# Sliding-window attention on one core: one masking with a difference of values, moved transposes and low parts, and another order of its end

## The chip, the core and the metric

The program runs on one core of a Trainium2 chip. Five engines work side by side, each through its own instructions in program order: TensorE (PE) multiplies matrices, VectorE (DVE), ScalarE (ACT) and GpSimd (POOL) work on elements, and SyncE (SP) issues most transfers. They wait for each other by semaphores. The metric is the device time of one execution in microseconds (us); the median of three runs before is 2189.2, from 2187.97 to 2191.01.

## The reference

A trunk of two layers over 1024 tokens of width 1024. The first layer mixes tokens by a gated linear recurrence, the second by the attention that the change touches; each is followed by a normalisation and a gated feed-forward block. The attention has 16 query heads and 4 shared key and value heads of 64. A query block of 128 tokens sees its own block and the one before, and of these only the 128 newest positions:

```python
t = jnp.arange(SW_WINDOW)[:, None] + SW_WINDOW
s = jnp.arange(2 * SW_WINDOW)[None, :]
dist = t - s
band = (dist >= 0) & (dist < SW_WINDOW)
...
logits = jnp.where(mask[None, :, None, None], logits, -jnp.inf)
m = jnp.maximum(logits.max(-1), sink)
p = jnp.exp(logits - m[..., None])
denom = p.sum(-1) + jnp.exp(sink - m)
o = jnp.einsum('bngrts,bnsgd->bntgrd', p, vv.astype(jnp.float32))
o = o / jnp.moveaxis(denom, -1, 2)[..., None]
```

So in a row of 256 logits exactly 128 count: of the own block the positions up to the query, of the previous block the positions behind it. Both halves fit into one square of 128 x 128.

## The kernel before

Large products are made in three: an operand is split into a high part (a cast on ACT) and a low part (what the cast lost, a subtraction on DVE, line 166), and high x high, high x low and low x high are summed (`mm3`, lines 191 to 193). Scores take a high and a low part of the keys; the attention's transposes (`tr`, line 201) and its products with the values (`mm32`, line 197) are in plain f32.

The attention runs over 8 values of `c` (a pair of query heads, one of each of two key heads) and 4 values of `bp` (two blocks of 128 tokens each): 32 steps, numbered here 0 to 31 as 4c + bp. `attend` is a generator that makes one step's work in seven stages:

1. scores on PE (line 1290) into a `psax` tile; ACT copies the own block's half to `X` (1293);
2. DVE lays the previous block's half over it where it counts (1297), POOL adds the bias (1303);
3. DVE takes the maximum (1308, 1311), ACT the exponentials with their sums (1315, 1317);
4. DVE adds the sink, takes the reciprocal and normalises `X` (1319 to 1321);
5. PE transposes the four squares of `X` into a `psmm` tile;
6. DVE multiplies this with each of two triangular masks (1329): `W[:, 0]` is the own block's part, `W[:, 1]` the previous block's;
7. PE multiplies with the values of the own and of the previous block (1338, 1340), ACT copies the result to column `c` of `Y` (1342), or for c = 7 splits it into `T` at once.

Four blocks are in flight. In a step the newest goes through stages 1 and 2, and the older ones through 3 and 4, 5 and 6, and 7. PE has a filler beside this: the projection of the next pair's queries (`q_proj`, two pieces of six products a step), and for c = 7 the beginnings of the output projection (`last_filler`). A finished half of the queries is split by `q_split` (1274, 1276) in every second step. `make_lows` lets out the low parts that were put off in `lows`: those of weights (`HL`), and in the last six steps those of finished columns of `Y`, which `Y_to_T` splits into `T` (`moves` says which columns in which step).

PE, ACT, DVE and POOL keep the order in which the code calls them here (`manual_schedule`), so the order of the `stage` calls in the step loop (lines 1408 to 1440) sets what stands behind what in each queue. After the loop the three blocks left over, 29 to 31, are finished by hand (lines 1441 to 1464), with pieces of the output projection (`out_part`) between their stages.

Of the kernel before, what the change touches and what calls it, by code (L numbers as in the profile page):

```python
# [10 lines left out]
F32 = mybir.dt.float32  # L11
# [5 lines left out]
P = 128  # L17
# [18 lines left out]
def constant_arrays():  # L36
    s = np.arange(P)[:, None]
    t = np.arange(P)[None, :]
    masks = np.zeros((P, 7 * BL + P), np.float32)
    bs, bt = s % BL, np.arange(BL)[None, :]  # L40
    pair = lambda m: (bs // (2 * m) == bt // (2 * m)) & (bs % (2 * m) < m) & (bt % (2 * m) >= m)
    parts = [bs == bt, pair(1), pair(2) & (bs % 4 == 0), pair(2) & (bs % 4 == 1)] + [pair(1 << i) for i in range(2, 5)]
    for i, part in enumerate(parts):
        masks[:, i * BL:(i + 1) * BL] = part
    masks[:, 7 * BL:] = t > s
    tri = np.zeros((P, 2, P), np.float32)
    tri[:, 0] = s <= t
    tri[:, 1] = s > t
    onehot = np.zeros((32, 2 * P), np.float32)
    for x in range(2 * P - 1):  # L50
        onehot[BUCKETS[(x - P + 1) % P], x] = 1.0
    return {"masks": masks, "tri": tri, "onehot": onehot}
# [55 lines left out]
def trunk(ctx: ExitStack, tc: tile.TileContext, a: dict, out: bass.AP):  # L108
# [87 lines left out]
    def mm32(ps, lhsT, rhs, start=True, stop=True, cost=0.218, **kw):  # L196
        nc.tensor.matmul(ps, lhsT, rhs, start=start, stop=stop, **kw)  # L197
        od.t += cost

    def tr(ps, src):  # L200
        nc.tensor.transpose(ps, src, ident)  # L201
        od.t += 0.109
# [989 lines left out]
    with (tc.tile_pool(name="ta", bufs=1, reuse_waits="tile") as raws,  # L1192
          tc.tile_pool(name="at", bufs=1, reuse_waits="tile") as at):
        raw_tail(raws)
        Kh = at.tile([P, 2, 2, S], F32R, name="Kh")
        tri = at.tile([P, 2, P], F32, name="tri")
# [4 lines left out]
        wkvv = wkv.rearrange("(kc p) c -> p kc c", p=P)  # L1201
        Kl = at.tile([P, 2, S], F32R, name="Kl")
        Vt = at.tile([P, NB, 256], F32, name="Vt")
        khl, uv = [], []
        for c in range(2):
            hl = split_into(hl_at(4 + c), load(lambda r: [(r.rearrange("p (k c) -> p k c", k=KC),
# [22 lines left out]
        def v_part(tp):  # L1229
            ps = psmm()  # L1230
            proj_tok(uv, tp, ps)
            nc.scalar.copy(Vt[:, 2 * tp:2 * tp + 2, :], ps.rearrange("p (a b) -> p a b", a=2))

        wq = a["swa_w_q"][0].rearrange("(kc p) (h e) -> p kc h e", p=P, e=64)

        W0 = at.tile([P, 2, 4, P], F32, name="W0")
        bfs = {}

        def bias_load(c):
# [39 lines left out]
        def attend(c, bp, q):  # L1279
# [43 lines left out]
            pt = psmm()  # L1323
            for i in range(4):
                tr(pt[:, i * P:(i + 1) * P], X[:, i // 2, i % 2, :])
            yield
            W = W0 if bp % 2 else Y[:, NB - 1, :].rearrange("p (k g s) -> p k g s", k=2, g=4)
            for k in range(2):
                nc.vector.tensor_tensor(W[:, k], pt.rearrange("p (g s) -> p g s", g=4),
                                        tri[:, k, :].unsqueeze(1).to_broadcast([P, 4, P]), op=ALU.mult)  # L1330
            yield
            po = psmm()
            for jj in range(2):
                j = 2 * bp + jj
                for e in range(2):
                    kvc = (2 * pp + e) * 64
                    o = po[64 * e:64 * e + 64, jj * P:(jj + 1) * P]
                    mm32(o, Vt[:, j, kvc:kvc + 64], W[:, 0, 2 * e + jj, :], stop=j == 0)
                    if j:
                        mm32(o, Vt[:, j - 1, kvc:kvc + 64], W[:, 1, 2 * e + jj, :], start=False)  # L1340
            if c < 7:
                nc.scalar.copy(Y[:, c, bp * 256:(bp + 1) * 256], po[:, :256])
            else:
                ts = slice(bp * 256, (bp + 1) * 256)
                split(T[:, 0, c, ts], T[:, 1, c, ts], po[:, :256], lows)
            yield

        wo2 = a["swa_w_out"][0]
# [32 lines left out]
        with tc.manual_schedule(engines={EN.PE, EN.Activation, EN.DVE, EN.Pool}):  # L1381
# [26 lines left out]
            for c in range(8):  # L1408
                fill = q_proj(hl) if c < 7 else last_filler()
                nq, nd = next(fill)  # L1410
                for bp in range(4):
                    it = attend(c, bp, q)
                    prev = [None] * (3 - len(flight)) + flight
                    if 4 * c + bp in moves:
                        Y_to_T(*moves[4 * c + bp], lows)
                    stage(it)
                    stage(prev[0])
                    stage(prev[2])
                    stage(it)
                    stage(prev[1])  # L1420
                    stage(prev[1])
                    stage(fill)
                    stage(prev[2])
                    while done:
                        q_split(*done.pop(0))
                    make_lows()
                    if bp == 0 and c < 6:
                        hl = q_unit(c + 2)
                    stage(fill)
# [69 lines left out]
```

## Time and profile before

| what | us |
|---|---|
| median of three runs | 2189.2 |
| the profiled execution | 2192.32 |
| its span | 2190.5 |
| the attention's steps 0 to 31 and its end (1276.0 to 1466.7 of the span) | 190.7 |
| PE busy in the whole span | 2168.1 |
| DVE busy in the whole span | 1762.2 |
| ACT busy in the whole span | 895.3 |

The profile is a page on one execution, with views of its trace. A timeline row gives the start, the duration, the engine, the line, the operation, out and in, shapes and a count; in brackets stands how long the engine sat idle before it and what ended that. Instructions that follow one another on an engine can overlap a little, so a pitch is the difference of two starts. A busy PE is not PE at its peak, since the ends of its products are modelled; there, too, starts tell more.

### The profile page before, as it was taken

To read this page: it belongs to the slowest core of one execution; us is meant where nothing else is said; L and a number is where in the kernel's file an instruction comes from. 1 tells how busy PE (TensorE), PEld (TensorE's weight loads), DVE (VectorE), ACT (ScalarE), POOL (GpSimd) and SP (SyncE) were. 2 spreads that over 40 slices of the span, in tenths; PEclk is the share of its full clock that TensorE was granted. 3 is DMA by queue.
4 is the path that set the end of the run, shared out by engine and by line. 5 is a ranking of instruction groups with operands and counts; after the bars stand their busy time and mean duration, and the time that the engine had idled before them with its cause. 6 is when DMAs were issued, how large, how long until landed. Compare 5 with 4: busy or idle time off the path is not lost.

```text
span 2190.5 us, 33214 instructions
## 1 busy us (share of the span) xinstructions
PE 2168.1 (99%) x13188; PEld 1813.6 (83%) x13188; DVE 1762.2 (80%) x2388; ACT 895.3 (41%) x1457; POOL 120.3 (5%) x135
## 2 busy tenths in 40 slices
PE   9999999999999999999999999999999999999998
PEld 8888888998888888888878888878888888888877
DVE  3776666667999988887978568969999988878986
ACT  3233333343444444444433256743544444434430
POOL 1000000000100000000001123211000000000001
PEclk9999999999999999999999999999999999999999
DMA  5654533305223222228854411133223222249662
GB/s 196 231 167 162 183 136 102 97 22 175 98 73 106 87 85 79 77 96 271 281 183 154 126 32 28 32 106 110 93 96 97 77 87 77 84 138 325 229 209 88
DMA packets 229844, 279.05 MB, mean 127 GB/s; under 512 B 29960, under 2 KB 158648, under 8 KB 226872
## 3 DMA queue, kind: packets, MB, share of 16 engines
q1 hardware_dynamic: 228736, 276.53, 38.7%
q8 instruction: 104, 1.70, 0.3%
q14 instruction: 52, 0.43, 0.1%
q10 hardware_dynamic: 856, 0.37, 0.1%
q0 software_dynamic: 96, 0.02, 0.0%
HBM read 213.94 MB, written 62.94 MB: 126 GB/s over the span
## 4 chain that ended last, share of the span: by engine, by line
PE 84%; DVE 9%; DMA 3%; issue 2%; ACT 2%; SPq 0%; POOL 0%; DVEq 0%; ACTq 0%; POOLq 0%
PE psmm L191 18%; PE psmm L193 17%; PE psmm L192 17%; PE psax L191 8%; PE psax L192 8%; PE psax L193 8%; PE psax L197 3%; DVE T L166 2%; PE psax L201 1%; DVE HL L166 1%; PE psmm L201 1%; PE psmm L197 1%; PE psax L1290 1%; DMA R<-bsd 1%; DMA rx<-gd 1%
## 5 line engine op out<-in xcount | busy, mean ns | idle before, releaser
L191 PE MATMUL psmm<-T,HL 128*128 128x512 f32 x768 | 307.4, 400 | 0.0
L192 PE MATMUL psmm<-T,HL 128*128 128x512 f32 x768 | 300.3, 391 | 0.0
L193 PE MATMUL psmm<-T,HL 128*128 128x512 f32 x768 | 300.2, 391 | 0.0
L470 DVE SCALAR_TENSOR_TENSOR Y<-Y,cwt 128x1023 f32<-128x1023 f32 (+1 forms) x176 | 225.1, 1281 | 43.3 <-ACT Y L468 39.9
L218 ACT CAST HL<-rx 128x1024 fp32r<-128x1024 f32 (+1 forms) x151 | 151.0, 1004 | 219.9 <-PE psmm L192 45.0
L191 PE MATMUL psmm<-HL,T 128*128 128x256 f32 (+1 forms) x656 | 198.3, 302 | 0.0
L193 PE MATMUL psmm<-HL,T 128*128 128x256 f32 (+1 forms) x656 | 194.3, 296 | 1.4 <-DVE T L166 1.4
L192 PE MATMUL psmm<-HL,T 128*128 128x256 f32 (+1 forms) x656 | 194.0, 296 | 0.0
L166 DVE TENSOR_TENSOR HL<-rx,HL 128x1024 fp32r<-128x1024 f32 (+1 forms) x151 | 174.4, 1161 | 19.1 <-ACT HL L218 18.9
L193 PEld LDWEIGHTS psmm<-T,HL 128*128 128x128 f32 x768 | 144.2, 188 | 31.3
L191 PEld LDWEIGHTS psmm<-T,HL 128*128 128x128 f32 x768 | 144.3, 188 | 30.6 <-issue 0.4
L192 PEld LDWEIGHTS psmm<-T,HL 128*128 128x128 f32 x768 | 144.4, 188 | 28.2
L468 ACT ACTIVATE Y<-Y,cwt 128x1024 f32<-128x1024 f32 x88 | 108.8, 1238 | 103.6 <-DVE Y L457 96.0
L192 PE MATMUL psax<-T,HL 128*128 128x512 f32 x352 | 137.8, 391 | 0.0
L191 PE MATMUL psax<-T,HL 128*128 128x512 f32 x352 | 137.7, 391 | 0.0
L193 PE MATMUL psax<-T,HL 128*128 128x512 f32 x352 | 137.4, 390 | 0.0
L191 PEld LDWEIGHTS psmm<-HL,T 128*128 128x128 f32 x656 | 125.3, 191 | 6.2 <-issue 2.5
L193 PEld LDWEIGHTS psmm<-HL,T 128*128 128x128 f32 x656 | 125.3, 191 | 5.2 <-DVE T L166 2.1
L192 PEld LDWEIGHTS psmm<-HL,T 128*128 128x128 f32 x656 | 125.4, 191 | 3.3
L240 POOL TENSOR_TENSOR rs<-rs,nhalf 128x1 f32<-128x1 f32 x32 | 45.6, 1424 | 1420.4 <-DVE rs L239 1420.4
L166 DVE TENSOR_TENSOR HL<-raw,HL 128x1024 fp32r<-128x1024 f32 x51 | 62.4, 1225 | 66.7 <-ACT HL L173 66.4
L191 PEld LDWEIGHTS psax<-T,HL 128*128 128x128 f32 x352 | 66.1, 188 | 14.6
(293 smaller groups left out, 5087.0 us busy)
## 6 DMA issues: line engine op xcount, KB each, us to landing
rx<-in_ffn_w_in_dram SPq DMA_DIRECT2D x136, 256.0 KB, 3.5
rx<-gd SPq DMA_DIRECT2D x118, 256.0 KB, 3.4
Y<-in_ffn_w_out_dram SPq DMA_DIRECT2D x44, 512.0 KB, 5.8
bsd<-Y SPq DMA_DIRECT2D x22, 1024.0 KB, 4.7
gd<-Y SPq DMA_DIRECT2D x44, 512.0 KB, 2.6
rx<-in_ffn_w_out_dram SPq DMA_DIRECT2D x54, 256.0 KB, 3.7
R<-bsd SPq DMA_DIRECT2D x44, 256.0 KB, 4.6
Y<-in_ffn_w_in_dram SPq DMA_DIRECT2D x40, 256.0 KB, 3.0
```

Source lines behind the costliest of these rows:

```text
L166: make = lambda e: e.tensor_tensor(lo, src, hi.bitcast(F32), op=ALU.subtract)
L191: nc.tensor.matmul(ps, st(0), mv(0), start=start, stop=False)
L192: nc.tensor.matmul(ps, st(0), mv(1), start=False, stop=False)
L193: nc.tensor.matmul(ps, st(1), mv(0), start=False, stop=stop)
L197: nc.tensor.matmul(ps, lhsT, rhs, start=start, stop=stop, **kw)
L201: nc.tensor.transpose(ps, src, ident)
L218: nc.scalar.copy(hi, src)
L240: nc.gpsimd.tensor_tensor(rs, rs, nhalf, op=ALU.pow)
L468: nc.scalar.activation(c, u, AF.Identity, bias=cwt[:, l, 3, ci:ci + 1], scale=cwt[:, l, 2, ci:ci + 1])
L470: nc.vector.scalar_tensor_tensor(c[:, sh:], u[:, :S - sh], cwt[:, l, 2 - sh, ci:ci + 1], c[:, sh:], op0=ALU.mult, op1=ALU.add)
L1290: nc.tensor.matmul(pv[:, e, jj, lo:], q[bp // 2][es, e, qs], Kl[es, pp, ks] if low else Kh[:, pp, e, ks], start=not low and jj == 0, stop= ...
```

## The change

The own block's mask and the previous block's mask add up to one everywhere. So with P for the transposed square, M for the own block's triangle, and V and V' for the own and the previous block's values, M P V + (1 - M) P V' is written as P V' + M P (V - V'). The second masking goes; ACT copies P out of PSUM in its place (into `X`, which is free by then), and `dV` holds the differences of values, made once on POOL as the values are projected. Products with values stay as many. The masked half lies in one half of `Y[:, 7]` by turns, so the tile `W0` goes.

In the step loop the order of the calls is new: `Y_to_T` comes after the new scores and the old values; `make_lows` comes ahead of the filler; the first piece of the filler comes ahead of the transposes, and the masking (with the copy) after the normalising of the next block. For c = 7 the low part of a values' result goes to the head of `lows`. The end has another order of stages and pieces.

```diff
-    tri = np.zeros((P, 2, P), np.float32)
-    tri[:, 0] = s <= t
-    tri[:, 1] = s > t
+    tri = (s <= t).astype(np.float32)
...
+        dV = at.tile([P, NB - 1, 256], F32, name="dV")
...
             nc.scalar.copy(Vt[:, 2 * tp:2 * tp + 2, :], ps.rearrange("p (a b) -> p a b", a=2))
+            b0 = max(2 * tp, 1)
+            nc.gpsimd.tensor_tensor(dV[:, b0 - 1:2 * tp + 1, :], Vt[:, b0:2 * tp + 2, :], Vt[:, b0 - 1:2 * tp + 1, :],
+                                    op=ALU.subtract)
...
-            W = W0 if bp % 2 else Y[:, NB - 1, :].rearrange("p (k g s) -> p k g s", k=2, g=4)
-            for k in range(2):
-                nc.vector.tensor_tensor(W[:, k], pt.rearrange("p (g s) -> p g s", g=4),
-                                        tri[:, k, :].unsqueeze(1).to_broadcast([P, 4, P]), op=ALU.mult)
+            X = X.rearrange("p e j s -> p (e j) s")
+            nc.scalar.copy(X, pt.rearrange("p (g s) -> p g s", g=4))
+            W = Y[:, NB - 1, :].rearrange("p (k g s) -> p k g s", k=2, g=4)[:, bp % 2]
+            nc.vector.tensor_tensor(W, pt.rearrange("p (g s) -> p g s", g=4),
+                                    tri.unsqueeze(1).to_broadcast([P, 4, P]), op=ALU.mult)
...
-                    mm32(o, Vt[:, j, kvc:kvc + 64], W[:, 0, 2 * e + jj, :], stop=j == 0)
                     if j:
-                        mm32(o, Vt[:, j - 1, kvc:kvc + 64], W[:, 1, 2 * e + jj, :], start=False)
+                        mm32(o, Vt[:, j - 1, kvc:kvc + 64], X[:, 2 * e + jj, :], stop=False)
+                    mm32(o, dV[:, j - 1, kvc:kvc + 64] if j else Vt[:, 0, kvc:kvc + 64], W[:, 2 * e + jj, :], start=j == 0)
...
-                split(T[:, 0, c, ts], T[:, 1, c, ts], po[:, :256], lows)
+                first = []
+                split(T[:, 0, c, ts], T[:, 1, c, ts], po[:, :256], first)
+                lows[:0] = first
...
+                    stage(it)
+                    stage(prev[0])
                     if 4 * c + bp in moves:
                         Y_to_T(*moves[4 * c + bp], lows)
-                    stage(it)
-                    stage(prev[0])
                     stage(prev[2])
                     stage(it)
+                    make_lows()
+                    stage(fill)
                     stage(prev[1])
+                    stage(prev[2])
                     stage(prev[1])
-                    stage(fill)
-                    stage(prev[2])
                     while done:
                         q_split(*done.pop(0))
-                    make_lows()
...
             next(a31)
             next(a29)
+            Y_to_T(4, 6, 4, 8, lows)
+            make_lows()
+            out_part(begun[2], us, 2, range(4))
             next(a30)
+            next(a31)
             next(a30)
+            out_part(begun[2], us, 2, range(4, 7))
+            out_part(begun[3], us, 3, range(2))
+            next(a30)
+            next(a31)
+            next(a31)
+            Y_to_T(6, 7, 4, 8, lows)
             make_lows()
-            out_part(begun[2], us, 2, range(6))
+            out_part(begun[3], us, 3, range(2, 7))
             next(a31)
             make_lows()
-            next(a30)
-            out_part(begun[2], us, 2, [6])
-            next(a31)
-            next(a31)
-            make_lows()
-            Y_to_T(4, 7, 4, 8)
-            out_part(begun[3], us, 3, range(4))
-            next(a31)
-            make_lows()
-            out_part(begun[3], us, 3, range(4, 7))
```

How the queues move shows in the instructions of two engines. DVE, from a split of queries (`q`) to the end of the next step; `dn` is the denominator, `nm` the negated maximum, `W` the tile `W0`. Before:

```order
L1276 SCALAR_TENSOR_TENSOR q<-psmm,q 64x512 x2
L1308 TENSOR_REDUCE nm<-X 128x4
L1311 SCALAR_TENSOR_TENSOR nm<-nm,nsk 128x4
L1297 COPY_PREDICATED X<-msk,psax 128x256 x2
L1329 TENSOR_TENSOR W_10064<-psmm,tri 128x512 x2
L1319 TENSOR_TENSOR dn<-dn,se 128x4
L1320 RECIPROCAL dn<-dn 128x4
L1321 TENSOR_TENSOR X<-X,dn 128x512
L166 TENSOR_TENSOR HL<-raw_10040,HL 128x1024
```

Changed (the lines have moved by one to three; 164 is the low part):

```order
L1277 SCALAR_TENSOR_TENSOR q<-psmm,q 64x512 x2
L1309 TENSOR_REDUCE nm<-X 128x4
L1312 SCALAR_TENSOR_TENSOR nm<-nm,nsk 128x4
L1298 COPY_PREDICATED X<-msk,psax 128x256 x2
L164 TENSOR_TENSOR HL<-raw_10040,HL 128x1024
L1320 TENSOR_TENSOR dn<-dn,se 128x4
L1321 RECIPROCAL dn<-dn 128x4
L1322 TENSOR_TENSOR X<-X,dn 128x512
L1332 TENSOR_TENSOR Y<-psmm,tri 128x512
```

Two maskings ahead of the denominator have become one behind the normalising, and the weights' low part stands ahead of the denominator. ACT, in a step of the last group in which columns of `Y` go to `T`. Before:

```order
L218 CAST T<-Y 128x2x512
L1293 COPY X<-psax 128x512
L1342 COPY Y<-psmm 128x256
L1315 ACTIVATE X,dn<-X,nm 128x128 x4
L1317 ACTIVATE se<-se 128x4
```

Changed:

```order
L1294 COPY X<-psax 128x512
L1345 COPY Y<-psmm 128x256
L216 CAST T<-Y 128x2x512
L1316 ACTIVATE X,dn<-X,nm 128x128 x4
L1318 ACTIVATE se<-se 128x4
L1330 COPY X<-psmm 128x512
```

The cast stood ahead of the scores' copy and now stands between the values' copy and the exponentials; the copy of the transposes follows the exponentials.

More of the change, by code (lines that the diff above doesn't have):

```diff
@@ L1195, in trunk @@
         Kh = at.tile([P, 2, 2, S], F32R, name="Kh")
-        tri = at.tile([P, 2, P], F32, name="tri")
+        tri = at.tile([P, P], F32, name="tri")
         nc.scalar.dma_start(tri, a["tri"])
@@ L1232, in v_part @@
             nc.scalar.copy(Vt[:, 2 * tp:2 * tp + 2, :], ps.rearrange("p (a b) -> p a b", a=2))
+            b0 = max(2 * tp, 1)
+            nc.gpsimd.tensor_tensor(dV[:, b0 - 1:2 * tp + 1, :], Vt[:, b0:2 * tp + 2, :], Vt[:, b0 - 1:2 * tp + 1, :],
+                                    op=ALU.subtract)
         wq = a["swa_w_q"][0].rearrange("(kc p) (h e) -> p kc h e", p=P, e=64)
-        W0 = at.tile([P, 2, 4, P], F32, name="W0")
         bfs = {}
```

## The prediction

> **What bounds the kernel now.** I read the page first, then the stretch in which the change works, cut by steps. In the windows view the columns are the stretch, its length, then busy us (and instructions) of PE, PEld, DVE, ACT and POOL, the granted clock, the DMA share and GB/s. A step is one pass of the loop over `bp`; it begins with the score products of L1290. The three stretches are steps 20 to 23, steps 24 to 30, and step 31 with the end.
>
> ```profile
> span 2190.5 us, 33214 instructions
> PE 2168.1 (99%) x13188; PEld 1813.6 (83%) x13188; DVE 1762.2 (80%) x2388; ACT 895.3 (41%) x1457; POOL 120.3 (5%) x135
> ...
> 1382.95:1403.99 21.04, 21.04 (x157) 17.28 (x156) 19.11 (x40) 15.51 (x50) 5.89 (x10) 1.00 0.16 42
> 1403.99:1444.92 40.93, 38.24 (x277) 30.61 (x276) 39.29 (x83) 28.05 (x92) 10.95 (x13) 1.00 0.06 16
> 1444.92:1466.71 21.79, 18.65 (x121) 14.42 (x119) 14.70 (x30) 7.55 (x27) 2.24 (x2) 0.84 0.32 109
> ```
>
> PE never rests in steps 20 to 23: four steps in 21.04, 5.26 us a step (5.31, and 5.10 where block 0 saves two value products). An edit there wins only by making PE's own work shorter. In steps 24 to 30, seven steps should take 7/4 of 21.04 = 36.8 and take 40.9: 4.1 us lost, with DVE busy 39.29 of 40.93. In the last stretch PE rests twice, and its clock falls:
>
> ```profile
> 1450.45 1.11 PE L197 MATMUL psmm<-W,Vt 128*64 128x128 f32 x16 [1.43 <-DVE W L1329]
> 1453.12 1.09 PE L201 MATMUL psmm<-ident,X 128*128 128x128 f32 x4 [1.55 <-DVE T L166]
> 1453.86 0.78 PE L191 MATMUL psax<-HL,T 128*128 128x512 f32 x1
> 1454.43 0.63 PE L192 MATMUL psax<-HL,T 128*128 128x512 f32 x1
> ...
> 1452.00:1453.00 1.00, 0.00 (x0) 0.00 (x0) 1.00 (x3) 0.00 (x0) 0.00 (x0) 0.50 0.00 0
> 1458.00:1459.00 1.00, 1.00 (x5) 0.76 (x4) 0.00 (x0) 0.00 (x0) 0.00 (x0) 0.59 0.00 0
> ```
>
> Two waits on DVE, 1.43 + 1.55 us. From 1452.0 to 1458.8 the clock is 0.50, and PE works in 5.7 us of that; a product takes 0.43 there against 0.23, so 2.7 us go. All that the change can find is 4.1 + 3.0 + 2.7, some 10 us (0.45%); the other 2,000 us stay.
>
> **Term A, transposes between two halves of the fill.** No product is added or dropped, but PE changes its kind of work once more a step. Before it goes values, transposes, fill; the end of the kernel already shows values, fill, transposes, fill:
>
> ```profile
> 1341.84 1.14 PE L197 MATMUL psmm<-W,Vt 128*64 128x128 f32 x16
> 1342.92 0.66 PE L201 MATMUL psmm<-ident,X 128*128 128x128 f32 x4
> 1343.33 0.48 PE L191 MATMUL psmm<-T,HL 128*128 128x512 f32 x1
> 1343.64 0.39 PE L192 MATMUL psmm<-T,HL 128*128 128x512 f32 x1
> ...
> 1460.47 1.15 PE L197 MATMUL psmm<-Y,Vt 128*64 128x128 f32 x16
> 1461.55 0.50 PE L191 MATMUL psax<-HL,T 128*128 128x512 f32 x1
> 1461.89 0.39 PE L192 MATMUL psax<-HL,T 128*128 128x512 f32 x1
> 1462.12 0.39 PE L193 MATMUL psax<-HL,T 128*128 128x512 f32 x1
> 1462.35 0.60 PE L201 MATMUL psmm<-ident,X 128*128 128x128 f32 x4
> 1462.70 0.48 PE L191 MATMUL psax<-HL,T 128*128 128x512 f32 x1
> 1463.02 0.39 PE L192 MATMUL psax<-HL,T 128*128 128x512 f32 x1
> ```
>
> From the values' start to the second fill product: 1343.64 - 1341.84 = 1.80. The new order, by starts: 1.08 + 0.34 + 0.23 + 0.35 + 0.32 = 2.32, which holds two ordinary fill products more (0.46): 1.86. So 0.06 a step, times 30 steps with transposes: **+1.8 us**. Bounds: 0 (one sample), and 3.3 if each switch costs the 0.11 that a first product takes over an ordinary one.
>
> **Term B, the new loop through ACT and DVE.** One masking (680 ns) leaves DVE in each step, and a copy of the transposes (as L1293's, 0.58) joins ACT, which was busy 15.5 of 21.04. That is not a cost by itself. But the order of DVE now puts the masking behind the normalising of the next block (L1319 to L1321), which waits for that block's exponentials on ACT; these stand behind the copy of the previous values' result (L1342). So values, copy, exponentials, normalising, masking, values is a closed loop, once a step. Its rows:
>
> ```profile
> 1343.02 0.37 ACT L1342 COPY Y<-psmm 128x256 f32<-128x256 f32 x1 [0.48 <-PE psmm L197]
> 1343.29 0.41 ACT L1315 ACTIVATE X<-X,nm 128x128 f32<-128x128 f32 x1
> ...
> 1345.07 0.16 DVE L1319 TENSOR_TENSOR dn<-dn,se 128x4 f32<-128x4 f32 x1 [0.17 <-ACT se L1317]
> 1345.27 0.18 DVE L1320 RECIPROCAL dn<-dn 128x4 f32<-128x4 f32 x1
> 1345.48 0.69 DVE L1321 TENSOR_TENSOR X<-X,dn 128x512 f32<-128x512 f32 x1
> 1346.20 1.41 DVE L1276 SCALAR_TENSOR_TENSOR q<-psmm,q 64x512 fp32r<-64x512 f32 x2
> 1347.64 0.69 DVE L1308 TENSOR_REDUCE nm<-X 128x4 f32<-128x512 f32 x1
> 1348.37 0.16 DVE L1311 SCALAR_TENSOR_TENSOR nm<-nm,nsk 128x4 f32<-128x4 f32 x1
> 1348.56 0.78 DVE L1297 COPY_PREDICATED X<-msk,psax 128x256 f32<-128x256 uint8 x2
> 1349.23 1.28 DVE L1329 TENSOR_TENSOR W<-psmm,tri 128x512 f32<-128x512 f32 x2
> 1350.43 0.37 DVE L1319 TENSOR_TENSOR dn<-dn,se 128x4 f32<-128x4 f32 x1
> 1350.83 0.18 DVE L1320 RECIPROCAL dn<-dn 128x4 f32<-128x4 f32 x1
> 1351.05 0.69 DVE L1321 TENSOR_TENSOR X<-X,dn 128x512 f32<-128x512 f32 x1
> 1351.65 1.22 DVE L166 TENSOR_TENSOR HL<-raw,HL 128x1024 fp32r<-128x1024 f32 x1
> 1352.79 0.68 DVE L1308 TENSOR_REDUCE nm<-X 128x4 f32<-128x512 f32 x1
> 1348.64 0.40 ACT L1315 ACTIVATE X<-X,nm 128x128 f32<-128x128 f32 x1
> ```
>
> A plain step: values to copy 1.18 (1341.84 to 1343.02), to the exponentials 0.27, to the normalising 1.78, through it 0.41 and 0.60 (1351.05 to 1351.65), the masking 0.68, PE's wake 0.14 (a masking ended 1450.31 by its rows, the values ran at 1450.45): 5.06. PE's step is 5.31 + 0.06 = 5.37: covered, with 0.31 in hand.
>
> Where the step before has split a query (L1276, every second step), that work stands behind the masking and ahead of the maximum. From masking to masking: -0.08 (overlap) + 1.44 (1346.20 to 1347.64) + 1.00 (maximum to exponentials at 1348.64) + 1.78 + 0.41 + 0.60 + 0.68 = 5.83; less the 0.31, 5.52. This falls on the step behind the short block-0 values, 5.37 - 0.22 = 5.15: 0.37 late. Every other time a weights' low part (1.14) now stands in it too, and DVE runs without a pause: -0.08 + 1.44 + 0.73 + 0.19 + 0.67 + 1.14 + 0.40 + 0.22 + 0.60 + 0.68 = 5.99, less 0.31, against 5.37: 0.31 late. Six of each in steps 2 to 25: 4.1. The masked operand is wanted only by the second product, 0.13 behind the first (two rows of 0.07), so each could be 0.13 less: 2.5. The output units' low parts in steps 22 to 25 add some 0.5. I take **+4.0**; bounds 0 (a loop 0.4 shorter than its rows) and 8 (0.3 longer).
>
> **Term C, steps 25 to 31.** The change moves the low parts under the exponentials and the cast of finished columns (L218 through `Y_to_T`) from ahead of the scores' copy to just ahead of the exponentials: into the loop.
>
> ```profile
> 1427.93 1.03 ACT L218 CAST T<-Y 128x1024 fp32r<-128x1024 f32 x1
> 1428.87 0.57 ACT L1293 COPY X<-psax 128x512 f32<-128x512 f32 x1
> ```
>
> 0.94 more: 6.00 a step against 5.37, 0.6 late; behind a query split DVE's own run is 6.2 (as above, with `se` on DVE, 0.2). Five passes: 0.5, 1.05, 0.5, 0.8 and 0.2 (half a cast) = 3.1. The 4.1 of today and the 0.24 by which step 31's values stretch go: **-1.2**. Bounds -4.3 (all hidden) and +1.
>
> **Term D, the end.** The wait of 1.55 is cured by taking the values' low part first. But the values of block 29 stand behind the same loop, with less fill over it: 1.18 + 0.28 (a small cast) + 0.94 + 1.78 + 0.41 + 0.60 + 0.68 = 5.9 after the values of 28, and PE has 1.07 + 0.80 + 0.35 + 0.78 = 3.0 of work by then. Idle 2.9, against 1.43 + 1.55: **-0.1**. The clock: two rests with 1.1 us of work between them halved it for 6.8 us; one rest of 2.9, then work without a pause, I let halve it for half as long, at 1.6 instead of 2.7: **-1.1**. Bounds -2.7 and +0.7.
>
> The page "TensorE: Matmul & The Clock Gate" of the Trainium skill, in "What's actually happening", has the clock halve after an idle window of about 3.4 us; the trace differs, since no rest here reached 1.6 us and it still halved, though 6.8 us is two such windows. By that rule the changed end, with 2.9 us, would keep its clock: that is the third rival.
>
> At nothing: the differences of values (four POOL operations in the projection; POOL is busy 5.89 of 21.04, and nothing waits on it there), ACT's copy (covered by the second half of the fill; 0.58 a step if not), the halved `tri`, and the queue of SP, whose order is unchanged (the residual's loads into `Y` wait for the end's last reads of it; the sums that need them come after 42 + 18 fill products at 0.23, 14 us).
>
> **Sum:** 1.8 + 4.0 - 1.2 - 0.1 - 1.1 = +3.4 us. The profiled execution took 2192.32, its span 2190.5, 3.1 over the median of 2189.2; added to the median: **2192.6**.
>
> **Rivals.** *The loop is longer than its rows* (27 in 100): ACT's copy and the masking now read one PSUM bank at once, which no row shows. From 0.3 us on, the hand of 0.31 is gone: 12 x 0.3 + 5 x 0.3 + 0.3 more: 2198. *The loop is shorter, or covers itself* (7): term B is 0, 2188.6. *The clock stays full* (9): 2192.6 - 1.6 = 2191.0. *Faster* (11): DVE, which ends every rest of PE today, has 0.68 less a step, and its low parts run early; if the exponentials start some 0.7 earlier than by L1342's copy, the loop with a split stays under 5.15, all waits vanish and the clock holds: -10 + 1.8 gives 2181; with the end's wait kept, 2184. Against it stands the order of ACT. That the change does not do what it says I exclude: the order shows it all.
>
> **How the numbers follow.** A difference of 0.2% (4.4 us) is about what a measurement of this kernel can tell. The forecast has 46 in 100, its own range 2190 to 2195.5, of which 26 lie within 0.2% and 20 above. Slower: 20 + 27 + 3 of the clock's case = 50. Within: 26 + 7 + 6 = 39. Faster: 11. The range, 2187 to 2199, leaves out most of the fast case and the worst of the slow one.
>
> **What would show it.** A: four steps in the middle of attention at 21.3 or more, and no row with values straight into transposes. B: the values (L195 there) waiting on DVE's masking in every second step, 0.1 to 0.4 each. C: 3 us of such waits in the last steps, no wait on a low part. D: one rest near 2.9 us ahead of block 29's values. Wrong if the values never wait in the middle steps, or if ACT's copy of the transposes ends after the masking.

## The result and the profile after

The changed kernel takes 2207.4 us (median of six runs, 2204.9 to 2209.9), the kernel before 2189.7 in the same series (2188.0 to 2191.0): a ratio of 1.0084, with a 95% interval from 1.0073 to 1.0094. It is 0.8% slower. The forecast of 2192.6 had the sign of its likeliest case right and a fifth of the size; 2207.4 lies outside its range (2187 to 2199).

The page of the profiled execution (2206.24 us) begins:

```profile
span 2204.4 us, 33210 instructions
PE 2174.8 (99%) x13188; PEld 1815.0 (82%) x13188; DVE 1754.4 (80%) x2357; ACT 911.5 (41%) x1490; POOL 133.3 (6%) x139
```

DVE is less busy than before, by 7.8 us, and the kernel is slower. Where the time went is told by the windows view, cut at the first score product of steps 3, 23 and 31 and at the end of the fill behind the last values. Before:

```profile
1293.69:1398.89 105.20, 105.20 (x781) 86.38 (x780) 95.79 (x206) 69.92 (x248) 32.53 (x50) 1.00 0.13 33
1398.89:1444.92 46.03, 43.34 (x313) 34.77 (x312) 44.23 (x91) 31.55 (x101) 11.82 (x14) 1.00 0.07 18
1444.92:1508.11 63.19, 60.05 (x300) 48.27 (x299) 44.53 (x73) 18.17 (x39) 3.77 (x3) 0.95 0.48 152
```

After:

```profile
1292.55:1408.58 116.03, 110.57 (x781) 87.91 (x780) 89.27 (x187) 80.43 (x267) 37.21 (x50) 1.00 0.12 30
1408.58:1460.40 51.82, 45.91 (x313) 36.46 (x312) 45.67 (x87) 35.92 (x111) 16.31 (x14) 0.97 0.09 30
1460.40:1521.07 60.67, 58.06 (x300) 46.23 (x298) 40.07 (x65) 19.06 (x39) 2.82 (x2) 1.00 0.46 139
```

PE has the same number of products in each (x781, x313, x300 here; the loads beside them to within one). Steps 3 to 22 are 10.8 us longer, steps 23 to 30 5.8 longer, step 31 with the end 2.5 shorter: +14.1 in all, and the spans differ by 13.9. POOL, which nothing in the change was meant to touch, is busy 4.7 us longer in the first stretch. The granted clock (the first number behind POOL's) takes part in the other two: 0.95 in before's last stretch, 0.97 in the changed kernel's steps 23 to 30.

Kernels with the same order of work take the same time in steps 3 to 22 to a few hundredths (before and e8 below; the changed kernel and e3), so the parts below are told by these stretches. The medians of runs differ by 17.7, 3.6 more than the stretches: the profiled execution of before lies 2.6 above its kernel's median, the changed one's 1.1 below. The former is an unlucky one by its clock: its mean of 0.997 is that of only six of the 75 other runs of before with a clock on record. Their median is 2190.5, that of the 41 with 0.999 is 2188.1.

PE's starts, step by step, show a pattern of four. A plain step takes 5.39 (5.32 before). Behind a step with bp 3 the values take 1.64 to the start of the fill, behind one with bp 1 2.23, where 1.07 is normal: 0.57 and 1.16 lost, five times each in steps 3 to 22 (the first pair somewhat more: 2.10 and 2.31). The wait is DVE's masking; in the PE timeline, one of each kind:

```profile
1323.16 0.32 PE L195 MATMUL psmm<-Y,dV 128*64 128x128 f32 x1 [0.19 <-DVE Y L1332]
1335.10 0.32 PE L195 MATMUL psmm<-Y,dV 128*64 128x128 f32 x1 [0.77 <-DVE Y L1332]
```

(The modelled ends of the products ahead of it hide a part of the wait.) DVE's timeline ahead of the longer one, with POOL's below it:

```profile
1328.79 0.69 DVE L1277 SCALAR_TENSOR_TENSOR q<-psmm,q 64x512 fp32r<-64x512 f32 x1
1329.52 0.69 DVE L1309 TENSOR_REDUCE nm<-X 128x4 f32<-128x512 f32 x1
1330.24 0.16 DVE L1312 SCALAR_TENSOR_TENSOR nm<-nm,nsk 128x4 f32<-128x4 f32 x1
1330.43 0.78 DVE L1298 COPY_PREDICATED X<-msk,psax 128x256 f32<-128x256 uint8 x2
1331.11 1.21 DVE L164 TENSOR_TENSOR HL<-raw,HL 128x1024 fp32r<-128x1024 f32 x1
1332.28 1.23 DVE L1320 TENSOR_TENSOR dn<-dn,se 128x4 f32<-128x4 f32 x1
1333.54 0.18 DVE L1321 RECIPROCAL dn<-dn 128x4 f32<-128x4 f32 x1
1333.75 0.69 DVE L1322 TENSOR_TENSOR X<-X,dn 128x512 f32<-128x512 f32 x1
1334.36 0.68 DVE L1332 TENSOR_TENSOR Y<-psmm,tri 128x512 f32<-128x512 f32 x1
```

```profile
1331.35 2.13 POOL L1304 TENSOR_TENSOR X<-X,bf 128x512 f32<-128x512 f32 x1 [0.67 <-DVE X L1298]
1336.66 1.29 POOL L1304 TENSOR_TENSOR X<-X,bf 128x512 f32<-128x512 f32 x1 [0.55 <-DVE X L1298]
```

Two rows stand out. POOL's bias add takes 2.13 us where the low part (L164) runs, and 1.29 elsewhere. The sum `dn` (L1320), four elements a partition, takes 1.23 us, and ends (1333.51) 0.03 behind the add's end (1333.48). Counting back from there, 1333.48 - 1.29 = 1332.19, which is 0.13 ahead of the low part's end (1332.32); and 1333.51 - 0.16 = 1333.35, 0.13 ahead of the add's end. To this 0.13 us, the add did its work only from the end of the low part on, and the sum only when the add was done. Three instructions that read two operands from SBUF have run one after the other, across two engines.

### The profile page after: what moved, and what is told of

Read it like the earlier page. It is cut to its first block, busy times and chain, and to the rows that moved or that the text cites. A ratio compares the mean times of both kernels' runs of the same rounds, so it can differ in the third digit from the quotient of the medians.

```text
span 2204.4 us, 33210 instructions
## 1 busy us (share of the span) xinstructions
PE 2174.8 (99%) x13188; PEld 1815.0 (82%) x13188; DVE 1754.4 (80%) x2357; ACT 911.5 (41%) x1490; POOL 133.3 (6%) x139
## 4 chain that ended last, share of the span: by engine, by line
PE 80%; DVE 11%; DMA 3%; ACT 3%; issue 2%; POOL 0%; SPq 0%; DVEq 0%; ACTq 0%; POOLq 0%
PE psmm L189 17%; PE psmm L191 16%; PE psmm L190 16%; PE psax L189 8%; PE psax L190 8%; PE psax L191 8%; PE psax L195 3%; DVE HL L164 1%; DVE T L164 1%; PE psax L199 1%; ACT X L1316 1%; DVE q L1277 1%; PE psmm L195 1%; DVE dn L1320 1%; DMA rx<-in_ffn_w_in_dram 1%
## 5 line engine op out<-in xcount | busy, mean ns | idle before, releaser
L164 DVE TENSOR_TENSOR HL<-rx,HL 128x1024 fp32r<-128x1024 f32 (+1 forms) x151 | 174.4, 1162 | 19.3 <-ACT HL L216 19.2
L466 ACT ACTIVATE Y<-Y,cwt 128x1024 f32<-128x1024 f32 x88 | 108.9, 1238 | 103.0 <-DVE Y L455 100.8
L164 DVE TENSOR_TENSOR HL<-raw,HL 128x1024 fp32r<-128x1024 f32 x51 | 62.4, 1225 | 66.4 <-ACT HL L171 66.2
L216 ACT CAST HT<-rx 128x1024 fp32r<-128x1024 f32 (+1 forms) x37 | 35.5, 959 | 108.5 <-DVE rx L422 77.8
```

The source lines that it names most:

```text
L164: make = lambda e: e.tensor_tensor(lo, src, hi.bitcast(F32), op=ALU.subtract)
L216: nc.scalar.copy(hi, src)
L466: nc.scalar.activation(c, u, AF.Identity, bias=cwt[:, l, 3, ci:ci + 1], scale=cwt[:, l, 2, ci:ci + 1])
```

## The experiments

Fourteen kernels. Times are medians; the ratio to runs of the kernel before on the same chip stands behind each.

### Is it the meeting with the add? Runs e4 and e1

e4 leaves the bias out of the bp 1 blocks:

```diff
-            nc.gpsimd.tensor_tensor(X, X, bv.unsqueeze(2).to_broadcast([P, 2, 2, P]), op=ALU.add)
+            if bp % 4 != 1:
+                nc.gpsimd.tensor_tensor(X, X, bv.unsqueeze(2).to_broadcast([P, 2, 2, P]), op=ALU.add)
```

> The changed kernel with POOL's bias add (L1304) left out in the steps with bp 1, where the weights' low part runs (so the scores of these blocks have no bias; the time of all else is kept). Theory P (port): dn is 0.2 or less in the steps with a low part instead of 1.23, the values behind them wait 0.1 to 0.35 instead of 1.16: 6 x 0.8 to 1.0 less, 5 to 6 us, 2201 to 2203. Theory S (dn is long because it waits for ACT's last exponential, or for the low part's results to drain): dn stays at 1.1 or more, time 2206 to 2208.

Measured: 2200.2 us, 1.0049 [1.0034, 1.0064]. The sum takes 0.16 in those steps, and the values behind them 1.15 instead of 2.23; the bp 3 ones stay at 1.64. Steps 3 to 22 fall from 116.0 to 110.8. Theory P holds (the time is 0.8 below its range), S falls.

e1 puts the low parts back behind the query split:

```diff
-                    make_lows()
                     stage(fill)
...
                         q_split(*done.pop(0))
+                    make_lows()
```

> The changed kernel with the low parts (L164, L166) put back behind the masking and the query split; all else as changed. Theory P (port): POOL's bias add and a DVE operation with two SBUF operands run one after the other, never together: the weights' low part holds up the add (2.13 instead of 1.29 us), and the add then holds up the 4-element sum dn (1.23 instead of 0.2). With the low part away from the add, the add is back at 1.3, dn at 0.4 or less, and the values' extra wait in the steps behind a bp 1 step (now 1.16) falls to 0.2 to 0.6; the low part itself still stands in the loop one masking later, so that the next step may lose up to 0.3. Sum over six of each, 2.5 to 5 us less: 2202 to 2205. Theory W (work): the 1.2 us of the low part itself is what the loop pays for, wherever it stands, and the length of dn is a waiting that only fills time: 2206 to 2208, the wait moves to the next step.

Measured: 2207.6 us, 1.0085 [1.0068, 1.0102]. Two groups of POOL's and DVE's lines over steps 3 to 22, mean ns behind the bar, first the changed kernel, then e1:

```profile
L1304 POOL TENSOR_TENSOR X<-X,bf 128x512 f32<-128x512 f32 x20 | 30.8, 1538 | 9.9 <-DVE X L1298 9.5
L1320 DVE TENSOR_TENSOR dn<-dn,se 128x4 f32<-128x4 f32 x20 | 10.0, 502 | 23.4 <-ACT se L1318 23.4
```

```profile
L1304 POOL TENSOR_TENSOR X<-X,bf 128x512 f32<-128x512 f32 x20 | 25.9, 1293 | 9.9 <-DVE X L1298 9.5
L1320 DVE TENSOR_TENSOR dn<-dn,se 128x4 f32<-128x4 f32 x20 | 6.1, 306 | 26.8 <-ACT se L1318 26.8
```

The add is free of the low part and the sum is short, as P says, yet the time is W's. In its old place the low part stands between one masking and the next maximum, where nothing covers it: the waits of 0.57 and 1.16 become 0.97, 0.33 and 0.25 (the last in the scores). So the lock, as I call it from here on, is what makes the low part dear under the exponentials, but moving the low part there was not what closed the loop.

### What closes the loop? Runs e2, e6, e9, e5, e7, e12

e2 takes the masking ahead of the next block's normalising:

```diff
                     stage(prev[1])
-                    stage(prev[2])
                     stage(prev[1])
+                    stage(prev[2])
```

> The changed kernel with the masking (and ACT's copy of the transposes) put ahead of the normalising of the next block, so that the masking waits for the transposes alone; the transposes stay between the halves of the fill, the low parts stay early. Theory L (the closed loop values, copy, exponentials, normalising, masking, values is what costs): the values never wait in steps 3 to 23, these 21 steps take 21 x 5.27 + 21 x 0.07 = 112.2 us or less instead of 121.2, the steps 24 to 30 lose 5 us or more of their 9: 2206.2 - 9 - 5 = 2192 by the profile, 2191 to 2194, and less (2186 to 2190) if the one masking fewer covers steps 24 to 30 wholly. The long dn rows (1.2) may remain, since the add still meets the low part; they would then cost nothing. Theory B (ACT's copy and the masking disturb each other in one PSUM bank, or the transposes in the middle of the fill cost more than 0.07): the waits or the longer step stay: 2200 or more.

Measured: 2195.5 us, 1.0029 [1.0018, 1.0039]. Between the two theories: steps 23 to 30 take 46.0, as before, but steps 3 to 22 112.15 against 105.20, with waits of 0.68 and 0.45 left. The trace names a new releaser. DVE's waits, then ACT's copy and DVE's masking in the timelines:

```profile
DVE Y L1332 <- ACT X L1330: 35.0, 30, 2.7
```

```profile
1347.74 0.57 ACT L1330 COPY X<-psmm 128x512 f32<-128x512 f32 x1
```

```profile
1348.34 0.69 DVE L1332 TENSOR_TENSOR Y<-psmm,tri 128x512 f32<-128x512 f32 x1 [1.94 <-ACT X L1330]
```

The masking starts 0.03 behind the end of ACT's copy; in 30 of 32 steps that copy is its releaser. In the program its semaphore is ACT's, not PE's: copy and masking read the same PSUM tile, and the one that is written second waits for the one written first. The Trainium skill says why a program would do so: in "PSUM — Partial Sum Buffer", "PSUM bank collisions raise a hardware error", two engines must not be in one bank at the same time, reads against reads included. No run here lets them meet. The copy stands behind the exponentials on ACT, so the loop was still closed.

e6 has the change's arithmetic alone (one masking, the copy, the differences of values) in the old order, loop and end; e9 is e6 with the masking written first:

```diff
-            nc.scalar.copy(X, pt.rearrange("p (g s) -> p g s", g=4))
             W = Y[:, NB - 1, :].rearrange("p (k g s) -> p k g s", k=2, g=4)[:, bp % 2]
             nc.vector.tensor_tensor(W, pt.rearrange("p (g s) -> p g s", g=4),
                                     tri.unsqueeze(1).to_broadcast([P, 4, P]), op=ALU.mult)
+            nc.scalar.copy(X, pt.rearrange("p (g s) -> p g s", g=4))
```

> The kernel before with the change's arithmetic alone: one masking, ACT's copy of the transposes, the differences of values; its order in the loop and at the end is that of before. Theory C (the masking's wait on ACT's copy closes the loop): from masking to masking behind a query split 1.0 + 1.44 + 1.0 + 1.78 + 0.57 + 0.68 - 0.08 = 6.4 us, against 5.3 with 0.3 in hand: the values wait 0.3 to 0.7 behind each split, with a weights' low part (1.2) in it up to 1.5; 5 to 12 us in all: 2194 to 2201. Theory O (only the new order costs; one masking fewer is DVE work saved): 2186 to 2190, no wait of the values in steps 3 to 23.

> The kernel of the run e6 (before with the change's arithmetic alone, 2212.7) with one edit: the masking ahead of ACT's copy of the transposes in the program, so that it waits for PE instead of for ACT. Theory C (the masking's wait on ACT's copy, which stands behind the exponentials, is what cost e6 its 23 us): no wait of the values on the masking in steps 3 to 23, 5.26 us a step as before; in steps 24 to 30, DVE has 0.68 less a step: 2186 to 2190. Theory N (the copy itself, 0.58 more on ACT a step, or the products with another operand, are what costs): 2200 or more.

Measured: e6 2212.7 us, 1.0111 [1.0090, 1.0131], worse than the change as a whole and than expected; e9 2190.3 us, 1.0008 [0.9999, 1.0017]. Two lines that change places are worth 22 us. Steps 3 to 22 in the windows view, e6 and e9:

```profile
1293.45:1410.10 116.65, 109.87 (x781) 87.85 (x780) 80.99 (x185) 78.20 (x263) 31.53 (x50) 1.00 0.10 26
```

```profile
1294.09:1399.29 105.20, 105.20 (x782) 86.38 (x780) 84.67 (x186) 80.02 (x267) 32.41 (x50) 1.00 0.13 31
```

In e9 DVE is busy 84.67 us there instead of before's 95.79, and PE gains nothing by it, since it never waited. In steps 23 to 30, where DVE was the limit, e9 takes 47.6 against 46.0: now the values wait for ACT's copy (3.3 us in three waits). The masking taken off DVE came back as a copy on ACT, which is late there.

e5 is e2 with the same two lines exchanged; e7 is e5 with the transposes, copy and masking back ahead of the fill:

```diff
                     make_lows()
+                    stage(prev[1])
+                    stage(prev[1])
                     stage(fill)
-                    stage(prev[1])
-                    stage(prev[1])
                     stage(prev[2])
```

> The kernel of the run e2 (masking ahead of the next block's normalising) with one thing more: in the program the masking now stands ahead of ACT's copy of the transposes, so that its semaphore wait is on PE's transposes instead of on that copy. Theory C (copy): in e2 the masking began 0.03 us behind the end of ACT's copy, which stands behind the exponentials; so the loop was still closed, by another way. With this edit it is open: the values of steps 3 to 23 wait nowhere for the masking, these 21 steps take at most 21 x 5.34 = 112.2 us (e2: 117.2), steps 24 to 30 40 or less, the long and short dn rows cost nothing: 2186 to 2190. Theory D (DVE has too much work behind a query split, and the masking is late whatever it waits for): waits of 0.4 to 0.7 behind the splits as in e2, 2194 to 2197.

> The kernel of the run e5 with the transposes (and the copy and masking of them) put back ahead of the fill, where before had them; the low parts stay under the exponentials, the cast and the end stay as changed. If PE's switch of work between the halves costs what the prediction's term A says (0.06 a step; the changed kernel shows 5.39 a plain step against 5.32), this is 1.5 to 2 us less than e5: 2184 to 2188. Rival: the masking now has less time from the transposes and is earlier in DVE's queue, ahead of the transposes' end in steps where DVE is late, so that the values wait again in steps with a low part: e5 plus 2 to 5.

Measured: e5 2194.3 us, 1.0030 [1.0018, 1.0041]; e7 2189.7 us, 1.0006 [0.9997, 1.0015], 1.7 above what was expected. By its time e5 is D's; by its trace the waits for the masking are gone from steps 3 to 22, and five waits of 0.46 for ACT's copy are left (109.1 us in all, of which 1.4 is the 0.07 a step for the transposes). What e5 wins there over e2 it loses in steps 23 to 30 (47.5) and the end (61.5 at a clock of 0.97, against 59.9 at 1.00), where ACT's copy is late. In e7 steps 3 to 22 take 105.20 again. So transposes between the halves cost 0.07 a step on PE and some 2.5 us more by what they make late.

e12 exchanges the two lines in the changed kernel and does nothing else:

> The changed kernel with the masking ahead of ACT's copy in the program and nothing else: on DVE the masking stays behind the next block's normalising. Theory L (in the changed kernel the normalising closes the loop, and the copy runs beside it): the masking runs when it did, but the copy now waits for it, and the values' first product needs the copy: 0.4 to 0.6 later in each of the twelve late steps and perhaps some in the others: 2211 to 2218. Theory C' (the masking's wait on the copy is what makes the changed kernel late): 2200 or less.

Measured: 2256.4 us, 1.0307 [1.0288, 1.0326]: L's sign, and seven times its size. ACT's copy now waits for a masking that waits for the normalising, and ACT's whole queue waits behind the copy: the next scores' copy, the next values' copy, the next exponentials. ACT, PE and DVE in turn:

```profile
1321.91 0.59 ACT L1333 COPY X<-psmm 128x512 f32<-128x512 f32 x1 [2.87 <-DVE Y L1331]
...
1322.55 0.80 PE L195 MATMUL psmm<-X,Vt 128*64 128x128 f32 x4 [2.46 <-ACT X L1333]
...
1326.71 0.16 DVE L1320 TENSOR_TENSOR dn<-dn,se 128x4 f32<-128x4 f32 x1 [2.92 <-ACT se L1318]
```

Each engine rests in turn for the next. The rests lower the clock, too: 0.989 and 0.986 in the two runs of e12, 0.996 to 0.998 in those of the changed kernel. My expectation priced the values' wait for the copy, and not what was queued behind the copy.

### The last steps and the end. Runs e3, e8, e10, e11

e3 puts the cast of finished columns back ahead of the scores:

```diff
+                    if 4 * c + bp in moves:
+                        Y_to_T(*moves[4 * c + bp], lows)
                     stage(it)
                     stage(prev[0])
-                    if 4 * c + bp in moves:
-                        Y_to_T(*moves[4 * c + bp], lows)
```

e8 is before with the change's end alone, that is the part of the diff behind `a29, a30, a31 = flight` and the three lines with `first`; e10 is e9 with the same end; e11 is e10 with the two lines of the cast moved behind the exponentials:

```diff
-                    if 4 * c + bp in moves:
-                        Y_to_T(*moves[4 * c + bp], lows)
                     stage(it)
                     stage(prev[0])
                     stage(prev[2])
                     stage(it)
+                    if 4 * c + bp in moves:
+                        Y_to_T(*moves[4 * c + bp], lows)
```

> The changed kernel with the cast of finished columns (L218, steps 26 to 31) put back ahead of the scores' copy. Theory A (in these steps ACT's cast is in the closed loop, as the prediction's term C has it): up to 0.94 less in four or five steps, 2 to 4 us less: 2203 to 2205. Theory D (there DVE, with the columns' low parts, the bias add in its way and the long dn, sets the loop; the exponentials are not what comes last): 2206 to 2208, and the dn rows of those steps stay as they are.

> The kernel before with the change's order at the end alone (behind the last step: the finished columns' casts and low parts taken earlier, the pieces of the last output sums dealt out anew, the values' low part first). By the prediction's term D 1.2 us less: 2188; by what the changed kernel shows for its last stretch (2.9 less than before's, with the clock at 1.00 there), 2186 to 2187. Rival: the last stretch of the changed kernel gained because its steps were late and its columns' low parts were done by then; in before's loop the end does not gain: 2189 to 2190.

> The kernel of the run e9 with the change's end. If the end gives what the stretch from the last step on showed in e8 (60.9 us against 63.2 with the same products), 2 us less than e9: 2183 to 2188. Rival: the columns' low parts are late in another way in this loop (as in e7, where the last fill waited 1.2 and 0.95): no less than e9.

> The kernel of the run e10 with the cast of finished columns (L218 of before, steps 26 to 31) behind the exponentials on ACT instead of ahead of the scores' copy; the low parts stay behind the query split. If ACT's cast ahead of the copies is what still holds up the steps 26 to 31 (before: 0.9 to 1.3 in single steps), 1 to 3 us less than e10: 2181 to 2186. Rival: DVE's low parts hold them up, not ACT: as e10, within 1 us.

| run | us | ratio to before | steps 23 to 30 | step 31 and end |
|---|---|---|---|---|
| e3 | 2207.0 | 1.0082 [1.0067, 1.0097] | 49.9 | 61.7 |
| e8 | 2188.3 | 1.0000 [0.9990, 1.0009] | 46.0 | 60.9 |
| e10 | 2190.7 | 1.0005 [0.9996, 1.0014] | 47.6 | 60.7 |
| e11 | 2192.5 | 1.0020 [1.0011, 1.0029] | 50.1 | 60.1 |

e3: the time is D's. Its steps 23 to 30 are 1.9 us shorter than the changed kernel's and its end 1.0 longer (61.7 against 60.7), but that is mostly the clock, which is half for 3.4 us in step 28 of the changed kernel and at the end of e3. Of the 1.9, 1.5 lie in step 28 (8.90 against 7.35), where the values rest equally long in both (1.57 and 1.59); only 0.4 in step 27 can be the cast's. e8: by the trace the end alone saves 2.3 us, with the clock full:

```profile
1444.04:1504.93 60.89, 57.78 (x300) 46.37 (x299) 45.58 (x75) 19.49 (x41) 3.78 (x3) 1.00 0.51 159
```

The runs show nothing of it (an interval of 2 us to either side): the 63.2 of before is that of the execution with the low clock, with 6.8 us at half clock in this stretch. e10 gains nothing over e9, as its rival had it, and e11 is slower: the cast now stands on ACT between the exponentials and the copy of the transposes, and in steps 23 to 30 the values wait 5.7 us for that copy, in five waits.

### How much in all hangs on the add? Runs e13 and e14

The add left out in every step, of the changed kernel and of before:

```diff
-            nc.gpsimd.tensor_tensor(X, X, bv.unsqueeze(2).to_broadcast([P, 2, 2, P]), op=ALU.add)
```

> The changed kernel with POOL's bias add (L1304) left out in every step (the scores have no bias). Theory P (the add and DVE's operations with two SBUF operands run one after the other, and the prediction's loop went wrong by this alone): dn is 0.17 in all steps; the values behind a bp 3 step wait 0.35 instead of 0.57, those behind a bp 1 step 0.1 instead of 1.16; steps 3 to 22 take 105.2 + 1.4 (transposes) + 5 x 0.45 = 108.9 instead of 116.0; steps 23 to 30 fall from 51.8 to 45 or 47, as the prediction's term C had them: 2207.4 - 7.1 - 5 to 7 = 2193 to 2195. Theory Q (steps 24 to 30 are late because ACT's cast and copy are in the loop, with or without the add): these steps stay above 49: 2198 to 2201.

> The kernel before with POOL's bias add left out in every step: the control for the run e13. In before the add meets the sum dn for 0.2 us in most steps, under work of PE that covers it: steps 3 to 23 stay at 5.26 each, the time within 1 us of before by theory P and by theory Q alike, steps 24 to 30 up to 1 us less.

Measured: e13 2196.9 us, 1.0036 [1.0023, 1.0049]; e14 2186.0 us, 0.9991 [0.9981, 1.0000]. e13 in the windows view:

```profile
1291.74:1400.94 109.20, 108.95 (x781) 87.65 (x780) 82.49 (x188) 80.49 (x267) 6.44 (x30) 1.00 0.10 26
1400.94:1446.77 45.83, 44.48 (x313) 35.29 (x312) 39.25 (x86) 36.06 (x111) 2.41 (x6) 1.00 0.10 33
1446.77:1507.01 60.24, 57.88 (x300) 46.38 (x299) 39.72 (x65) 19.07 (x39) 1.47 (x1) 1.00 0.46 140
```

By the stretches theory P holds within 0.3 us (108.9 and 45 to 47 were expected) and Q falls. The values wait 0.34 behind bp 3 and 0.09 behind bp 1. In e14 steps 3 to 22 stay at 105.20 and steps 23 to 30 fall by 0.9 to 45.09. So in steps 3 to 30 the change costs 16.6 us with the add and 4.7 without: 11.9 hang on the add in the profiled executions. The runs are less plain: by their medians the change costs 10.9 without the add (2196.9 against 2186.0) and 17.7 with it, so that 6.8 hang on the add, each median's ratio being known to 2 or 3 us. e13's profiled execution, 2192.75, is the fastest of its six and the only one with a clock of 0.999 (the others 0.998), and its median is 2 to 4 us above P's expectation; e14's median is 2.9 below before's in the same series, where 1 was expected. What differs there lies in executions that no trace here shows.

## Why the prediction was wrong

**Term A, the transposes: right.** 0.06 a step forecast, 0.07 measured. That the copy behind them becomes late (e5) it did not see; in the changed kernel the masking is later still and covers it.

**Term B, the loop: right mechanism, wrong size, and this is the step that failed.** The loop through values, copy, exponentials, normalising and masking is there, late only behind a query split, as forecast: predicted 5.83 and 5.99 us from masking to masking, measured 6.17 (1316.93 to 1323.10 by their ends) and 7.01 (1328.03 to 1335.04). Of +4.0 us it made 9.4 in steps 3 to 22 (10.8 less 1.4 for A). The failed sentence is the sum "... + 1.14 + 0.40 + 0.22 + ...": the low part was entered at its own duration and the denominator behind it at 0.40, as though POOL did not matter (of POOL the prediction says that nothing waits on it). From the denominator's start to the reciprocal's it took 1.26 there, and 0.44 in the other loop, where 0.20 was entered. Without the add (e13) both loops take 5.93 to 5.96, near the two sums, and they lose 2.6 us: the rows of before were enough for all but the meeting. The clue stood in the quoted rows, unread: `dn` at 0.16 and 0.37 us for the same four elements. The longer ones end with POOL's add, in before as well; the add beside the `dn` of 1350.43 to 1350.80 ended at 1350.77:

```profile
1349.48 1.29 POOL L1303 TENSOR_TENSOR X<-X,bf 128x512 f32<-128x512 f32 x1 [0.68 <-DVE X L1297]
```

**Term C, steps 24 to 30: wrong sign, for the same reason.** -1.2 forecast, +5.8 measured, and without the add +0.7 (e13 against e14; steps 23 to 30, with 0.6 of A in it). In every second of these steps a low part of columns or weights meets the add, which then takes 2.1 us, and the denominator behind it 1.2. Of the 5.8, 1.5 are the half clock behind the rest of step 28, as e3's step 28 shows; no term had a loss of clock there.

**Term D, the end: right sign, and much of it luck.** -1.2 forecast, -2.5 measured. Not one rest of 2.9 but two, and the clock kept full. By the windows rows PE's idle time fell from 3.14 to 2.61 us and its busy time, at the same products, from 60.05 to 58.06: 0.5 are rests, 2.0 the clock. But before's half clock is that of its profiled execution. The control e14, with before's order and the clock full, needs no longer than the changed kernel:

```profile
1441.56:1501.17 59.61, 57.34 (x300) 46.23 (x299) 43.59 (x73) 18.08 (x36) 1.46 (x1) 1.00 0.51 161
```

(e14 has no adds, and its rests are 0.9 shorter than before's.) PE's rows and the clock in the changed kernel:

```profile
1465.96 0.43 PE L195 MATMUL psmm<-X,Vt 128*64 128x128 f32 x2 [1.49 <-ACT X L1330]
1467.32 0.32 PE L195 MATMUL psmm<-Y,dV 128*64 128x128 f32 x1 [0.93 <-DVE Y L1332]
```

```profile
1467.00:1468.00 1.00, 0.68 (x12) 0.68 (x13) 0.97 (x3) 0.00 (x0) 0.00 (x0) 1.00 0.75 193
```

**The rivals.** The one that came nearest (2198: copy and masking read one PSUM bank at once) had the wrong mechanism: they never read at once, since the program puts one behind the other. That wait is real and dear (e6 against e9), but the changed kernel hides it: the copy of 0.57 runs beside the 1.0 to 2.0 of the normalising, and only one wait of the masking is put down to it. The fast case needed a masking early enough to open the loop; no version with the masking behind ACT's copy (e2, e6) opened it. At nothing stood ACT's copy; that held in steps 3 to 22 and not at the end, where the values wait 1.49 for it (above).

**What stays open:** how much of the 17.7 hangs on the add (11.9 in the profiled executions, 6.8 by the medians), and whether the clock accounts for all of the scatter between executions. No version beat the kernel before by more than its interval; e8 is level with it.

## What to carry to other kernels

A transfer of work off an engine that PE does not wait for wins nothing, and a second engine that reads the same PSUM tile adds a wait: ask which of two readers is written first, and what stands behind the second one in its queue. Before an instruction with two SBUF operands is moved on DVE, look for what POOL does at that time; a tiny instruction whose duration has two values in the trace, the longer one ending with another engine's instruction, is a wait that the profile counts as busy. A loop's price by the rows of before holds only as far as its neighbours on other engines stay the same.

## What the runs showed of the hardware

- POOL's add (both operands in SBUF) and DVE's two-operand instructions from SBUF exclude each other for a whole instruction (to 0.13 us), and the one that starts second waits: the add 2.13 instead of 1.29 us behind the low part, the four-element sum 1.23 instead of 0.16 behind the add, and in e7 the low part itself, where the add started first (1428.54 to 1429.82):

```profile
1428.78 2.12 DVE L164 TENSOR_TENSOR T<-Y,T 128x1024 fp32r<-128x1024 f32 x1 [0.38 <-ACT T L216]
```

  The waiting is part of the busy time, and no releaser is named. Before's maskings, which read one operand from PSUM, kept their length beside the add (1.28 for two, from 1349.23, with the add of 1349.48). The Trainium skill has this rule in "SBUF — State Buffer", "Who interferes with whom": a DVE instruction with two SBUF inputs contends with a GpSimd instruction that reads SBUF, and the second to issue blocks fully. The runs agree with it; the prediction had not weighed it.
- The clock does not go by the length of a rest alone, but by windows on a fixed grid. In the sixteen traces every change of the granted clock comes a whole number of 3.413 us behind the first one, which lies 5.95 to 8.71 us into the span. The program's last microseconds aside, each of the 16 windows at full clock in which PE was idle for more than 1.84 us was followed by a window at half clock, and none in which it was idle for less than 1.57; in between, 8 were followed by one and 5 were not. So a rest counts by where the grid cuts it, and the grid lies otherwise in each execution. In step 28 the changed kernel has a rest of 1.57 and e3 one of 1.59:

```profile
1442.18 0.40 PE L195 MATMUL psmm<-Y,dV 128*64 128x128 f32 x1 [1.57 <-DVE Y L1332]
```

```profile
1443.87 0.32 PE L195 MATMUL psmm<-Y,dV 128*64 128x128 f32 x1 [1.59 <-DVE Y L1332]
```

  The grid's windows there, first the changed kernel's, then e3's:

```profile
1438.89:1442.30 3.41, 1.83 (x15) 1.24 (x15) 3.34 (x6) 1.32 (x5) 2.60 (x3) 1.00 0.01 2
1442.30:1445.71 3.41, 3.41 (x18) 2.79 (x19) 1.38 (x6) 1.58 (x4) 1.27 (x1) 0.50 0.00 0
```

```profile
1440.00:1443.41 3.41, 2.28 (x15) 1.59 (x13) 3.34 (x5) 2.74 (x8) 2.71 (x3) 1.00 0.00 0
1443.41:1446.83 3.42, 2.96 (x25) 2.48 (x26) 2.85 (x7) 1.83 (x10) 1.68 (x2) 1.00 0.01 2
```

  The changed kernel's rest lies in one window, and the next one is at half clock. e3's is cut at 1443.41, and its clock stays full. The rests of 1.49 and 0.93 at the end fall into two windows as well:

```profile
1462.78:1466.19 3.41, 1.92 (x12) 1.26 (x10) 2.96 (x7) 3.13 (x12) 1.28 (x1) 1.00 0.00 0
1466.19:1469.60 3.41, 2.48 (x21) 1.90 (x20) 1.99 (x5) 1.45 (x7) 0.00 (x0) 1.00 0.82 261
```

  So the third rival of the prediction came true at the end, but not by the rule it was drawn from, the idle window of about 3.4 us of the Trainium skill ("TensorE: Matmul & The Clock Gate", "What's actually happening"): the runs show its length as the grid's pitch, and that a window with less than half of it idle can be enough.
